# Hybrid attention and recurrence layer: output rows 8 to 11 taken into the fill, other buffers and queues for the end, first keys loaded earlier

## The chip, the cores and the metric

The kernel runs on one core of one Trainium2 chip. The metric is the device time of one execution in microseconds (us). The core has TensorE (PE), VectorE (DVE), ScalarE (ACT), GpSimd (POOL) and SyncE (SP), each with an instruction order that is fixed when the program is built. Before the change every DMA of the kernel is issued by SP, one after the other.

## What is computed

One layer of a decoder trunk over 2048 tokens of width 1024, in float32. Eight heads of differential attention and a gated linear recurrence (RG-LRU) run side by side; their outputs, 1024 wide each, go through one output projection.

```python
h = rmsnorm(x, pre_norm_g[l])
proj = jnp.einsum('bsd,de->bse', h, w_in[l])
q, k, v, g_attn, x_lru, g_lru = jnp.split(proj, SPLIT_POINTS, axis=-1)
...
    p = jax.nn.softmax(jnp.where(causal, s, -jnp.inf), axis=-1)
    w = p[:, :, 0] - lam * p[:, :, 1]
    outs.append(jnp.einsum('bhqk,bkhe->bqhe', w, v[:, :end].astype(jnp.float32)))
...
o = rmsnorm(o, subln_g[l]) * (1.0 - lam_init)
y_attn = o.reshape(B, S, ATTN_WIDTH).astype(x.dtype) * jax.nn.silu(g_attn)
xc = causal_depthwise_conv(x_lru, conv_w[l], conv_b[l])
hr = rg_lru(xc, w_r[l], b_r[l], w_i[l], b_i[l], lru_lambda[l])
y_lru = hr.astype(x.dtype) * jax.nn.silu(g_lru)
y = jnp.einsum('bse,ed->bsd', jnp.concatenate([y_attn, y_lru], axis=-1), w_out[l])
x = x + rmsnorm(y, post_norm_g[l])
```

## The kernel before

Every large product splits its float32 operands into a high and a low part and takes three matmuls of 128x512 (high by high, low by high, high by low). The work comes in stages, for the first half of the tokens (A) and the second (B): projections, the recurrence (`lru_run`, whose last piece is called as `end()`), and attention over four pairs of query rows (`range(0, 4)`, then `range(4, 8)`). Queries, keys, values, gates and the outputs `ya_s` (attention) and `yl_s` (recurrence) go through DRAM.

`attention` (L591) is a loop over slots. A slot belongs to a unit (head h, pair pr, tile t, component c), 128 of them in B, and twelve more slots follow the last unit. In a slot the code writes down, in this order: loads (keys L599, queries L615, values, gates), the exponentials of the unit (L679, ACT), then a mix of the next unit's score matmuls (L640) with their maxima (DVE), transposes of weights ("T", L711, whose low part `wl` is made by DVE), products with values ("V", L734) and **fill**, and at last the steps of the norm of a head and block j of 512 rows: `norm1` to `norm6`, "N1" to "N6" (L742 to L783). These steps are a square sum on PE (`pm`, L756), small operations on DVE (`f`), a trip through DRAM that spreads the result over the partitions (`r_s`, `rb`), a product on POOL (L779) and the store to `ya_s` (L782).

Fill is other PE work that comes from a generator, so many matmuls a slot: `FA` = 10 in A (projections of the second half), `FB` = 8.25 in B. B's fill is the output projection, `fill_out` (L1018), in 49 groups of 24 matmuls (L1045). A group (r, nh, i) multiplies the rows 128 i to 128 i + 127 of the recurrence's (r = 1) or attention's (r = 0) output by one half (nh = 0 left, nh = 1 right) of the columns of `w_out`. The order is (1,0), (1,1) for 16 rows each, then (0,0), (0,1) for the rows 0 to 7 that attention A has finished, then (0,1) of row 8. At the change from one set to the next, 8 pieces of weights are loaded (L947, two buffers) and split on POOL. All groups use one PSUM bank (`ps_f`). Partial sums go to DRAM (`part_s`) and come back (`part`, `yv`). When the right half of a row i below 8 is added (L1055), `finish` (L962) normalises the row of 1024 columns in the buffer `yv` (one buffer), adds x and stores it.

What is left stands in `p3`: the right halves of rows 9 to 15 and the left halves of rows 8 to 15 (`right` L1103, `left` L1110, matmuls L1095), with left weights that are loaded by SP into two buffers (L1120) and split between the right halves of rows 9, 10 and 11.

Memory pools lie on a left and a right side of SBUF; a tile in memory that another pool has given up waits for its last reader. A scheduler, which puts instructions mostly in the order in which the code gives them, fixes each engine's order, so a DMA can stand some rows away from its place in the code.

Of the kernel before, what the change touches and what calls it, by code (L numbers as in the profile page):

```python
# [8 lines left out]
F32 = mybir.dt.float32  # L9
# [34 lines left out]
def hymba_kernel(  # L44
# [342 lines left out]

    lightA = [light("k", 0), light("q", 0), light("g", 0)]
# [12 lines left out]
    with tc.tile_pool(name="ps_p", bufs=4, space=PSUM) as ps_p:  # L401
# [161 lines left out]
        with tc.tile_pool(name="lruA", bufs=2) as lp, tc.tile_pool(name="ps_g", bufs=1, space=PSUM) as ps_g:  # L563
# [3 lines left out]
            for job in jobs[5:]:  # L567
# [16 lines left out]
                pos += 2  # L584
            end()
    pA.close()

    def attention(prs, kv_p, e_p, a_p, ps_s, ps_w, ps_o, nsb, fill, per_slot, kbufs, vbufs, p1bufs):  # L591
        NS = len(prs)
        nmax = (prs[-1] + 1) * 256
        kst, vst, qst, gst, lch, wts = {}, {}, {}, {}, {}, {}

        def load_k(h, j):
            t = kv_p.tile([P, 2, CH], F32R, tag="ks", name="ks", bufs=kbufs)
            for e in range(2):
                nc.sync.dma_start(out=t[64 * e:64 * e + 64].bitcast(F32), in_=k_s[h][j][:, e])  # L599
            kst[h, j] = t  # L600

        def load_v(h, j):
            c0 = (h % 4) * P
            t = a_p.tile([P, 2, 4, P], F32R, tag="vs", name="vs", bufs=vbufs)
            nc.sync.dma_start(
                out=t.bitcast(F32).rearrange("p e t c -> p (e t) c"),
                in_=v_s[h // 4][j][:, :, :, c0:c0 + P].rearrange("p e t c -> p (e t) c"),
            )
            vst[h, j] = t[:, 0], t[:, 1]

        def load_q(h, pr):
            t0 = (pr % 2) * 256
            t = kv_p.tile([P, 2, 2, 256], F32R, tag="qs", name="qs", bufs=2)
            for r in range(2):
                nc.sync.dma_start(  # L615
                    out=t[64 * r:64 * r + 64].bitcast(F32), in_=q_s[h][pr // 2][:, :, :, t0:t0 + 256],
                )
            qst[h, pr] = t[:, 0], t[:, 1]

        def load_g(h, j):  # L620
            t = a_p.tile([P, CH], F32, tag="gt", name="gt", bufs=2)
            nc.sync.dma_start(out=t, in_=g_s[h][j])
            gst[h, j] = t


        def pieces(u):
            n = (2 * u[1] + u[2] + 1) * P
            return n, [(c0, min(n, c0 + SP)) for c0 in range(0, n, SP)]

        sc, negm, pex = {}, {}, {}  # L630

        def score_mm(u, pi):
            h, pr, t, c = u
            n, pcs = pieces(u)
            c0, c1 = pcs[pi]
            ps = ps_s.tile([P, SP], F32, tag="s", name="s")
            for b0 in range(c0, c1, CH):
                nk = max(256, min(CH, c1 - b0))
                for m, qq in enumerate(qst[h, pr]):
                    nc.tensor.matmul(  # L640
                        out=ps[:, b0 - c0:b0 - c0 + nk], lhsT=qq[:, c, t * P:(t + 1) * P],
                        rhs=kst[h, b0 // CH][:, c, 0:nk], start=(m == 0), stop=(m == 1),
                    )
            sc[u, pi] = ps

        def score_max(u, pi):
            n, pcs = pieces(u)
            c0, c1 = pcs[pi]
            if pi == 0:
                negm[u] = e_p.tile([P, 1], F32, tag="nm", name="nm", bufs=4)  # L650
            if pi == 0:
                sc[u, "mx"] = e_p.tile([P, 4], F32, tag="mx", name="mx", bufs=4)
            mx = sc[u, "mx"]
            s = sc[u, pi][:, 0:c1 - c0]
            if pi < len(pcs) - 1:
                nc.vector.tensor_reduce(out=mx[:, pi:pi + 1], in_=s, axis=AX.X, op=ALU.max)  # L656
                return

            nc.vector.tensor_tensor_reduce(
                out=s, in0=s, in1=mask16[:, CH - (c1 - c0):], scale=1.0, scalar=MASKED, op0=ALU.add, op1=ALU.max,  # L660
                accum_out=mx[:, pi:pi + 1],
            )
            nc.vector.tensor_reduce(out=negm[u], in_=mx[:, 0:pi + 1], axis=AX.X, op=ALU.max, negate=True)  # L663

        def score_exp(u):
            h, pr, t, c = u
            n, pcs = pieces(u)
            p = e_p.tile([P, nmax], F32, tag=f"p{c}", name=f"p{c}", bufs=(5, p1bufs)[c])
            pex[u] = p
            if (h, pr // 2) not in lch:  # L670
                lch[h, pr // 2] = e_p.tile([P, 4, 2], F32, tag="lch", name="lch", bufs=3)
            if c == 0 and len(pcs) > 1:
                sc[u[:3]] = e_p.tile([P, 2, 4], F32, tag="ls", name="ls", bufs=3)
            for pi, (c0, c1) in enumerate(pcs):
                if len(pcs) == 1:
                    acc = lch[h, pr // 2][:, (2 * pr + t) % 4, c:c + 1]
                else:
                    acc = sc[u[:3]][:, c, pi:pi + 1]
                nc.scalar.activation(  # L679
                    out=p[:, c0:c1], in_=sc.pop((u, pi))[:, 0:c1 - c0], func=AF.Exp, bias=negm[u], accum_out=acc,  # L680
                )

        def combine(h, pr, t):

            n, pcs = pieces((h, pr, t, 0))
            l2 = lch[h, pr // 2][:, (2 * pr + t) % 4, :]
            if len(pcs) > 1:
                nc.vector.tensor_reduce(
                    out=l2, in_=sc.pop((h, pr, t))[:, :, 0:len(pcs)], axis=AX.X, op=ALU.add,
                )  # L690
            rr = e_p.tile([P, 2], F32, tag="rr", name="rr", bufs=3)
            nc.vector.reciprocal(out=rr[:, 0:1], in_=l2[:, 1:2])
            nc.vector.scalar_tensor_tensor(
                out=rr[:, 1:2], in0=l2[:, 0:1], scalar=neglam, in1=rr[:, 0:1], op0=ALU.mult, op1=ALU.mult,
            )
            p0, p1 = pex.pop((h, pr, t, 0)), pex.pop((h, pr, t, 1))
            nc.vector.scalar_tensor_tensor(  # L697
                out=p0[:, 0:n], in0=p1[:, 0:n], scalar=rr[:, 1:2], in1=p0[:, 0:n], op0=ALU.mult, op1=ALU.add,
            )
            wts[h, pr, t] = p0  # L700


        tw, po = {}, {}

        def transpose_w(h, pr, b):
            pw = ps_w.tile([P, CH], F32, tag="pw", name="pw")
            cells = [(2 * b, 0), (2 * b, 1), (2 * b + 1, 0), (2 * b + 1, 1)]
            if b == pr:
                cells.pop(2)
            for i, (kb, t) in enumerate(cells):  # L710
                nc.tensor.transpose(pw[:, i * P:(i + 1) * P], wts[h, pr, t][:, kb * P:(kb + 1) * P], ident)  # L711
            n = len(cells) * P
            wh = a_p.tile([P, CH], F32R, tag="wh", name="wh", bufs=WB)
            wl = a_p.tile([P, CH], F32R, tag="wl", name="wl", bufs=WB)
            nc.scalar.activation(out=wh[:, 0:n], in_=pw[:, 0:n], func=AF.Copy)  # L715
            nc.vector.tensor_tensor(  # L716
                out=wl[:, 0:n], in0=pw[:, 0:n], in1=wh[:, 0:n].bitcast(F32), op=ALU.subtract,
            )
            tw[h, pr, b] = (wh, wl)

        def values(h, pr, b, e):
            j = pr // 2
            if pr % 2 == 0 and b == 0 and e == 0:
                po[h, j] = ps_o.tile([P, CH], F32, tag="o", name="o")
            wh, wl = tw[h, pr, b]
            o0 = (pr % 2) * 256
            kb = 2 * b + e
            vh, vl = vst[h, kb // 4]
            if b == pr and e == 1:
                w0, w1, oo = 256, 384, o0 + P  # L730
            else:
                w0, w1, oo = 256 * e, 256 * e + 256, o0
            for m, (a, w) in enumerate(((vh, wh), (vl, wh), (vh, wl))):
                nc.tensor.matmul(  # L734
                    out=po[h, j][:, oo:oo + w1 - w0], lhsT=a[:, kb % 4, :], rhs=w[:, w0:w1],
                    start=(kb == 0 and m == 0), stop=(kb == 2 * pr + 1 and m == 2),
                )


        nrm = {}  # L740

        def norm1(h, j):  # L742
# [49 lines left out]
        for p in range(H * NS):  # L792
# [16 lines left out]
            if p:  # L809
                later(s0 - 4, "Q", h, pr)  # L810
# [354 lines left out]
```

## Time and profile before

| | |
|---|---|
| median of 3 runs | 2257.87 us (2254.19 to 2262.12) |
| profiled execution, own time | 2261.0 us |
| its span in the profile | 2259.2 us |
| mean granted clock of PE | 0.983 |
| recurrence A, then attention A | from about 300 and 603 us |
| attention B: first score to last transpose of weights | 1379.3 to 2123.4 us |
| first matmul of `p3` (L1095) to the last | 2160.0 to 2250.5 us |

The page gives busy times by engine and the costliest groups of instructions. A row of the waits reads: engine, line, what it waited for, then the sum, the number and the longest of the waits in us. A row of the windows gives a stretch, its length and the busy time of each engine with its number of instructions. Matmuls overlap in the records: one of 128x512 shows about 390 ns, and the next starts 0.23 us after it.

### The profile page before, as it was taken

To read this page: it belongs to the slowest core of one execution; us is meant where nothing else is said; L and a number is where in the kernel's file an instruction comes from. 1 tells how busy PE (TensorE), PEld (TensorE's weight loads), DVE (VectorE), ACT (ScalarE), POOL (GpSimd) and SP (SyncE) were. 2 spreads that over 40 slices of the span, in tenths; PEclk is the share of its full clock that TensorE was granted. 3 is DMA by queue.
4 is the path that set the end of the run, shared out by engine and by line. 5 is a ranking of instruction groups with operands and counts; after the bars stand their busy time and mean duration, and the time that the engine had idled before them with its cause. 6 is when DMAs were issued, how large, how long until landed. Compare 5 with 4: busy or idle time off the path is not lost. (4 is left out here: it accounts for less than half of the span.)

```text
span 2259.2 us, 31702 instructions
## 1 busy us (share of the span) xinstructions
PE 2157.4 (95%) x11025; PEld 1792.9 (79%) x11025; DVE 1507.1 (67%) x3296; ACT 985.2 (44%) x2227; POOL 820.9 (36%) x773
## 2 busy tenths in 40 slices
PE   7999999999899999999999997999999998998888
PEld 7888888888678888888878775888788887887766
DVE  6531145546576767677347776888888887898775
ACT  4211134444454434444226565666556554555211
POOL 1223044434411111111366553223543235355542
PEclk9999999999999999999999998999999999999899
DMA  6554332332567665664552207456465455654473
GB/s 213 148 155 149 106 98 80 101 95 82 142 171 206 165 173 167 186 164 131 141 172 67 62 33 186 120 136 158 128 165 153 113 150 141 172 148 134 150 241 130
DMA packets 346497, 317.93 MB, mean 141 GB/s; under 512 B 20257, under 2 KB 278370, under 8 KB 346338
## 3 DMA queue, kind: packets, MB, share of 16 engines
q1 hardware_dynamic: 346338, 315.91, 50.0%
q8 instruction: 87, 1.43, 0.3%
q14 instruction: 72, 0.59, 0.1%
HBM read 221.41 MB, written 94.44 MB: 140 GB/s over the span
## 5 line engine op out<-in xcount | busy, mean ns | idle before, releaser
L227 PE MATMUL ps<-hh,whi 128*128 128x512 f32 (+1 forms) x1456 | 564.3, 388 | 0.0
L227 PE MATMUL ps<-hh,wlo 128*128 128x512 f32 (+1 forms) x1456 | 563.7, 387 | 0.0
L227 PE MATMUL ps<-hl,whi 128*128 128x512 f32 (+1 forms) x1456 | 562.5, 386 | 0.0
L679 ACT ACTIVATE p<-s,nm 128x512 f32<-128x512 f32 (+3 forms) x640 | 392.1, 623 | 342.1 <-DVE nm L663 295.4
L199 POOL TENSOR_TENSOR wlo<-wraw,whi 128x1024 fp32r<-128x1024 f32 x88 | 222.5, 2528 | 524.7 <-PE ps L227 187.6
L640 PE MATMUL s<-ks,qs 128*128 128x512 f32 (+2 forms) x1280 | 370.3, 387 | 29.8 <-DMA ks<-k_s 14.2
L656 DVE TENSOR_REDUCE mx<-s 128x1 f32<-128x512 f32 x384 | 258.6, 685 | 90.4 <-PE s L640 89.4
L227 PEld LDWEIGHTS ps<-hl,whi 128*128 128x128 f32 x1456 | 275.8, 189 | 51.6
L227 PEld LDWEIGHTS ps<-hh,wlo 128*128 128x128 f32 x1456 | 275.4, 189 | 51.2
L227 PEld LDWEIGHTS ps<-hh,whi 128*128 128x128 f32 x1456 | 276.0, 190 | 50.5
L640 PEld LDWEIGHTS s<-ks,qs 128*128 128x128 f32 x1280 | 213.0, 191 | 87.6 <-ACT p L679 44.2
L715 ACT ACTIVATE wh<-pw 128x512 fp32r<-128x512 f32 (+1 forms) x288 | 160.0, 577 | 164.1 <-PE pw L711 161.3
L70 POOL TENSOR_SCALAR yh<-yraw 128x256 fp32r<-128x256 f32 x196 | 95.0, 501 | 358.1 <-PE f L1045 357.8
L734 PE MATMUL o<-wh,vs 128*128 128x256 f32 (+1 forms) x1152 | 220.3, 283 | 0.6 <-ACT wh L715 0.6
L734 PEld LDWEIGHTS o<-wh,vs 128*128 128x128 f32 x1152 | 193.9, 192 | 18.5 <-ACT wh L715 2.6
L716 DVE TENSOR_TENSOR wl<-pw,wh 128x512 fp32r<-128x512 f32 (+1 forms) x288 | 185.9, 654 | 31.6 <-ACT wh L715 29.7
L697 DVE SCALAR_TENSOR_TENSOR p<-p,rr,p 128x128 f32<-128x128 f32 (+15 forms) x128 | 184.0, 1437 | 2.9
L711 PE MATMUL pw<-ident,p 128*128 128x128 f32 x1088 | 172.5, 275 | 8.5 <-DVE wl L716 6.3
L1045 PE MATMUL f<-woh,yh 128*128 128x512 f32 x392 | 161.7, 413 | 14.1 <-DVE yv L1055 7.6
L734 PE MATMUL o<-wl,vs 128*128 128x256 f32 x576 | 164.6, 286 | 5.5 <-DVE wl L716 5.0
L711 PEld LDWEIGHTS pw<-ident,p 128*128 128x128 f32 x1088 | 134.9, 141 | 42.2 <-issue 8.2
L1045 PE MATMUL f<-wol,yh 128*128 128x512 f32 x392 | 162.2, 414 | 0.0
(165 smaller groups left out, 3286.9 us busy)
## 6 DMA issues: line engine op xcount, KB each, us to landing
wraw<-in_w_in_dram SPq DMA_DIRECT2D x96, 512.0 KB, 4.7
qs<-q_s SPq DMA_DIRECT2D x128, 256.0 KB, 4.8
vs<-v_s SPq DMA_DIRECT2D x48, 512.0 KB, 5.1
ks<-k_s SPq DMA_DIRECT2D x96, 256.0 KB, 5.5
xt<-in_x_dram SPq DMA_DIRECT2D x32, 512.0 KB, 4.1
k_s<-hilo SPq DMA_DIRECT2D x64, 256.0 KB, 3.4
q_s<-hilo SPq DMA_DIRECT2D x64, 256.0 KB, 3.5
v_s<-hilo SPq DMA_DIRECT2D x32, 512.0 KB, 4.4
```

Of the source, the lines that this page charges most:

```text
L70: nc.gpsimd.tensor_scalar(out=hi, in0=src, scalar1=1.0, scalar2=1.0, op0=ALU.mult, op1=ALU.mult)
L199: nc.gpsimd.tensor_tensor(out=lo, in0=src, in1=hi.bitcast(F32), op=ALU.subtract)
L227: nc.tensor.matmul(out=ps[:, t0:t0 + n], lhsT=a[:, k, :], rhs=b[:, k, t0:t0 + n], start=(k == 0 and m == 0), stop=(k == KC - 1 and m == 2),)
L640: nc.tensor.matmul(out=ps[:, b0 - c0:b0 - c0 + nk], lhsT=qq[:, c, t * P:(t + 1) * P], rhs=kst[h, b0 // CH][:, c, 0:nk], start=(m == 0), st ...
L656: nc.vector.tensor_reduce(out=mx[:, pi:pi + 1], in_=s, axis=AX.X, op=ALU.max)
L679: nc.scalar.activation(out=p[:, c0:c1], in_=sc.pop((u, pi))[:, 0:c1 - c0], func=AF.Exp, bias=negm[u], accum_out=acc,)
L697: nc.vector.scalar_tensor_tensor(out=p0[:, 0:n], in0=p1[:, 0:n], scalar=rr[:, 1:2], in1=p0[:, 0:n], op0=ALU.mult, op1=ALU.add,)
L711: nc.tensor.transpose(pw[:, i * P:(i + 1) * P], wts[h, pr, t][:, kb * P:(kb + 1) * P], ident)
L715: nc.scalar.activation(out=wh[:, 0:n], in_=pw[:, 0:n], func=AF.Copy)
L716: nc.vector.tensor_tensor(out=wl[:, 0:n], in0=pw[:, 0:n], in1=wh[:, 0:n].bitcast(F32), op=ALU.subtract,)
L734: nc.tensor.matmul(out=po[h, j][:, oo:oo + w1 - w0], lhsT=a[:, kb % 4, :], rhs=w[:, w0:w1], start=(kb == 0 and m == 0), stop=(kb == 2 * pr ...
L1045: nc.tensor.matmul(out=ps, lhsT=a[:, k, :], rhs=b, start=(k == 0 and m == 0), stop=(k == 7 and m == 2),)
```

## The change

1. `attention` becomes a generator: it asks for the first keys and queries, yields, and then goes on as before. `attention_of` opens its pool and takes this first step; it is called ahead of the last `end()` of each recurrence. The pool of A's keys moves to the right side, where the projections' `pA` is closed earlier.
2. The fill of B is 9.4 a slot instead of 8.25, and ends with four groups (0,1,8) to (0,1,11), after row 7. Each waits, without holding up the slots, until the last head's "N6" of its block has been written down. They add the partial sum and store the right half back to `part_s`; the rows are finished in `p3`.
3. `yv` gets two buffers in a pool of its own.
4. In `p3` the left weights are loaded by ACT's DMA queue into eight buffers, the high part is made by ACT and the low part by DVE. The rights of rows 12 to 15 come first, then left 12, 8, 13, 9, 14, 10, 15, 11. The first half of `finish` moves from `right` to `left`. The pool lies on the right side; its split rows have five buffers instead of six.

```diff
+        for h, j in early:
+            load_k(h, j)
+        load_q(0, prs[0])
+        yield
+        e_p, a_p, ps_s, ps_w, ps_o, fill = pools
...
+                    elif r == "wait":
+                        nf = 0
...
+            gen = attention(range(4, 8), kv_p, pools, 4 * CH // SP, lambda s: 9.4 if s > 1 else 6, 6, 5, 1)
+        next(gen)
...
+            pA.close()
+            attA = attention_of("A")
             end()
-    pA.close()
...
         p1.close()
+        attB = attention_of("B")
         end()
...
-        groups = [(r, nh, i) for r, nh in wsets for i in range((8, 16)[r])] + [(0, 1, 8)]
+        v_p = pb.enter_context(tc.tile_pool(name="rowB", bufs=2, side="right"))
+        groups = [(r, nh, i) for r, nh in wsets for i in range((8, 16)[r])] + [(0, 1, i) for i in range(8, 12)]
...
+                if ysp is None:
+                    while (H - 1, i // 4) not in ya_done:
+                        yield "wait"
+                    ysp, parts = load_y(r, i)
...
-                if r == 0 and nh == 1:
+                if r == 0 and nh == 1 and i < 8:
                     nc.vector.tensor_tensor(out=yv[:, CH:], in0=ps, in1=part, op=ALU.add)
-                    ends[i] = finish(f_p, i, yv, 1, 1, nc.gpsimd if i < FE else nc.vector)
-                    if i < 8:
-                        ends.pop(i)()
+                    finish(f_p, i, yv, 1, 1, nc.gpsimd)()
...
+                        nc.sync.dma_start(
+                            out=part_s[1][i][:, CH:] if i >= 8 else part_s[0][i][:, 0:CH], in_=st,
+                        )
...
-        y_p = p3.enter_context(tc.tile_pool(name="y", bufs=2))
+        y_p = p3.enter_context(tc.tile_pool(name="y", bufs=2, side="right"))
...
+        def load_w0(k):
+            raw = y_p.tile([P, CH], F32, tag="woraw3", name="woraw3", bufs=8)
+            nc.scalar.dma_start(out=raw, in_=w_out2[k * P:(k + 1) * P, 0:CH])
+            return raw
+
+        def split_w0(k, raw):
...
+            nc.scalar.activation(out=hi, in_=raw, func=AF.Copy)
+            nc.vector.tensor_tensor(out=lo, in0=raw, in1=hi.bitcast(F32), op=ALU.subtract)
...
-        for i in range(9, 12):
...
-        for i in range(8, 16):
+        for i in range(12, 16):
...
             right(i)
...
+        for i in range(8, 12):
+            left(i + 4)
...
             left(i)
```

Three places show how the engines' orders move. The first is SP's order where attention A begins, before and after; `ks` and `qs` are the first keys and queries, `yl_s` the recurrence's stores, `vs` and `gt` values and gates, `hilo` stores of projected values:

```order
L343 DMA yl_s_201<-tg 128x512
L194 DMA wraw<-in_w_in_dram 128x8x128
L599 DMA ks<-k_s_0_92 64x1024 x2
L615 DMA qs<-q_s_0_60 64x4x256 x4
L599 DMA ks<-k_s_1_93 64x1024 x2
```

```order
L402 DMA ks<-k_s_0_92 64x1024 x2
L418 DMA qs<-q_s_0_60 64x4x256
L343 DMA yl_s_200<-tg 128x512
L418 DMA qs<-q_s_0_60 64x4x256 x3
L402 DMA ks<-k_s_1_93 64x1024
L343 DMA yl_s_201<-tg 128x512
```

The first keys stood behind the last store of the recurrence and stand ahead of its last two now.

The second is SP's order at the switch to the third set of output weights, (0,0), before and after. `woraw` are the weights, `yraw` rows of y, `part_s_15` the last partial sum of the set before; `k_s_0_116` to `k_s_2_118` are the keys of head 6, which u96 uses first:

```order
L947 DMA woraw<-in_w_out_dram 128x512
L955 DMA yraw<-ya_s_196 128x8x128
L947 DMA woraw<-in_w_out_dram 128x512 x6
L1066 DMA part_s_15_227<-fo 128x512
L947 DMA woraw<-in_w_out_dram 128x512
L955 DMA yraw<-ya_s_196 128x8x128
L599 DMA ks<-k_s_2_118 64x1024 x2
```

```order
L971 DMA woraw<-in_w_out_dram 128x512 x2
L585 DMA ya_s_198<-yt 128x512
L402 DMA ks<-k_s_0_116 64x1024
L971 DMA woraw<-in_w_out_dram 128x512 x2
L402 DMA ks<-k_s_0_116 64x1024
L402 DMA ks<-k_s_1_117 64x1024
L971 DMA woraw<-in_w_out_dram 128x512 x2
```

Before, the last keys of head 6 stood right behind the eight loads of weights; after, the loads stand between keys of the same head that are asked for earlier, and `k_s_2_118` comes 23 rows behind the last pair of loads.

The third is PE's order at the last `pm` of the kernel, the square sum of head 7 and block 3 (`norm2`), before and after. L1045 is fill (rows 6 to 8 behind `pm`), o (L734, after the change L537) products with values, ps_y (L1123 after the change) the matmuls of `p3`, the first of row 12:

```order
L734 MATMUL o<-wh,vs 128x128 x2
L734 MATMUL o<-wl,vs 128x128
L1045 MATMUL f<-woh_20086,yh 128x512
L1045 MATMUL f<-woh_20086,yl 128x512
L1045 MATMUL f<-wol_20087,yh 128x512
L756 MATMUL pm<-ones_235,sq 128x2 x4
L1045 MATMUL f<-woh_19911,yh 128x512
L1045 MATMUL f<-woh_19911,yl 128x512
```

```order
L537 MATMUL o<-wl,vs 128x128
L559 MATMUL pm<-ones_235,sq 128x2 x4
L1123 MATMUL ps_y<-woh_19202,yh_21597 128x512
L1123 MATMUL ps_y<-woh_19202,yl_21598 128x512
L1123 MATMUL ps_y<-wol_19203,yh_21597 128x512
```

Before, the fill of rows 6, 7 and 8 (72 matmuls) and then the rights of 9, 10 and 11 followed `pm`; after, the fill of rows 8 to 11 (96 matmuls) stands ahead of it, among the last products with values, and row 12 follows.

More of the change, by code (lines that the diff above doesn't have):

```diff
@@ L388, in hymba_kernel, with attention_of @@
+    def attention_of(half):
+        st = ExitStack()
+        kv_p = st.enter_context(tc.tile_pool(name="kv" + half, bufs=2, side="right"))
+        pools = []
+        if half == "A":
+            gen = attention(range(0, 4), kv_p, pools, NSA, lambda s: FA, 4, 4, 2)
+        else:
+            gen = attention(range(4, 8), kv_p, pools, 4 * CH // SP, lambda s: 9.4 if s > 1 else 6, 6, 5, 1)
+        next(gen)
+        return st, pools, gen
     lightA = [light("k", 0), light("q", 0), light("g", 0)]
@@ L898, in hymba_kernel @@
     with ExitStack() as pa:
-        kv_p = pa.enter_context(tc.tile_pool(name="kvA", bufs=2))
+        pkv, pools, run_attention = attA
+        pa.callback(pkv.close)
         e_p = pa.enter_context(tc.tile_pool(name="expA", bufs=2))
@@ L933, in fill_proj @@
                     yield "group"
-        attention(range(0, 4), kv_p, e_p, a_p, ps_s, ps_w, ps_o, NSA, fill_proj(), lambda s: FA, 4, 4, 2)
+        pools += [e_p, a_p, ps_s, ps_w, ps_o, fill_proj()]
+        for _ in run_attention:
+            pass
     pst.close()
@@ L1008, in hymba_kernel @@
     with ExitStack() as pb:
-        kvB_p = pb.enter_context(tc.tile_pool(name="kvB", bufs=2, side="right"))
+        pkv, pools, run_attention = attB
+        pb.callback(pkv.close)
         e_p = pb.enter_context(tc.tile_pool(name="expB", bufs=2, side="right"))
@@ L1023, in fill_out @@
             for g, (r, nh, i) in enumerate(groups):
+                if ysp is None:
+                    while (H - 1, i // 4) not in ya_done:
+                        yield "wait"
+                    ysp, parts = load_y(r, i)
+                    for p in parts:
+                        split(*p)
                 ps = ps_f.tile([P, CH], F32, tag="f", name="f")
@@ L1026, in fill_out @@
                 nxt = groups[g + 1] if g + 1 < len(groups) else None
-                if nxt:
+                ysp, parts = None, ()
+                if nxt and (nxt[0] or nxt[2] < 8 or (H - 1, nxt[2] // 4) in ya_done):
                     ysp, parts = load_y(*nxt[::2])
@@ L1030, in fill_out @@
                 c0 = nh * CH
-                if i >= 8 and r == 0:
-                    yv = f_p.tile([P, D], F32, tag="yv", name="yv", bufs=1)
-                    nc.sync.dma_start(out=yv, in_=part_s[1][i])
-                    part = yv[:, CH:]
-                    ys[i], yvs[i] = ysp, yv
-                elif r == 0:
-                    if nh:
-                        yv = f_p.tile([P, D], F32, tag="yv", name="yv", bufs=1)
+                if r == 0:
+                    if nh and i < 8:
+                        yv = v_p.tile([P, D], F32, tag="yv", name="yv")
                         nc.sync.dma_start(out=yv[:, 0:CH], in_=part_s[0][i][:, 0:CH])
@@ L1067, in fill_out @@
                 yield "group"
-        attention(
-            range(4, 8), kvB_p, e_p, a_p, ps_s, ps_w, ps_o, 4 * CH // SP, fill_out(),
-            lambda s: FB if s > 1 else 6, 6, 5, 1,
-        )
+        pools += [e_p, a_p, ps_s, ps_w, ps_o, fill_out()]
+        for _ in run_attention:
+            pass
     with ExitStack() as p3:
-        y_p = p3.enter_context(tc.tile_pool(name="y", bufs=2))
+        y_p = p3.enter_context(tc.tile_pool(name="y", bufs=2, side="right"))
         ps_y = p3.enter_context(tc.tile_pool(name="ps_y", bufs=6, space=PSUM))
@@ L1083, in load_ya @@
             nc.sync.dma_start(out=raw, in_=ya_s[i // 4][:, :, (i % 4) * P:(i % 4 + 1) * P])
-            yh = y_p.tile([P, 8, P], F32R, tag="yh3", name="yh3", bufs=6)
-            yl = y_p.tile([P, 8, P], F32R, tag="yl3", name="yl3", bufs=6)
+            yh = y_p.tile([P, 8, P], F32R, tag="yh3", name="yh3", bufs=5)
+            yl = y_p.tile([P, 8, P], F32R, tag="yl3", name="yl3", bufs=5)
             split3(yh, yl, raw, SY)
@@ L1101, in hymba_kernel, with begin, right @@
         w0 = []
-        def right(i):
+        def load_w0(k):
[3 more added lines that the diff above has]
+        def split_w0(k, raw):
+            hi = y_p.tile([P, CH], F32R, name=f"w3h{k}", bufs=1)
+            lo = y_p.tile([P, CH], F32R, name=f"w3l{k}", bufs=1)
+            nc.scalar.activation(out=hi, in_=raw, func=AF.Copy)
+            nc.vector.tensor_tensor(out=lo, in0=raw, in1=hi.bitcast(F32), op=ALU.subtract)
+            w0.append((hi, lo))
+        def begin(i):
             yvs[i] = y_p.tile([P, D], F32, tag="yv3", name="yv3", bufs=5)
             nc.sync.dma_start(out=yvs[i], in_=part_s[1][i])
+        def right(i):
             ps = out_mm(i, w1)
             nc.vector.tensor_tensor(out=yvs[i][:, CH:], in0=ps, in1=yvs[i][:, CH:], op=ALU.add)
-            ends[i] = finish(y_p, i, yvs[i], 2, 1 + (i == 15), nc.vector if FY else nc.gpsimd)
         def left(i):
+            ends[i] = finish(y_p, i, yvs[i], 2, 1 + (i == 11), nc.gpsimd)
             ps = out_mm(i, w0)
@@ L1113, in left @@
             ends.pop(i)()
-        load_ya(9)
-        load_ya(10)
-        for i in range(9, 12):
-            for k in ((0, 1, 2), (3, 4, 5), (6, 7))[i - 9]:
-                raw = y_p.tile([P, CH], F32, tag="woraw3", name="woraw3")
-                nc.sync.dma_start(out=raw, in_=w_out2[k * P:(k + 1) * P, 0:CH])
-                hi = y_p.tile([P, CH], F32R, name=f"w3h{k}", bufs=1)
-                lo = y_p.tile([P, CH], F32R, name=f"w3l{k}", bufs=1)
-                split3(hi, lo, raw, SW)
-                w0.append((hi, lo))
-            right(i)
-            load_ya(i + 2)
-        for i in range(8, 16):
+        raws = [load_w0(k) for k in range(8)]
+        for k, raw in enumerate(raws):
+            split_w0(k, raw)
+        load_ya(12)
+        load_ya(13)
+        begin(12)
+        begin(13)
+        for i in range(12, 16):
+            if i < 14:
+                load_ya(i + 2)
+                begin(i + 2)
+            elif i == 14:
+                load_ya(8)
+                begin(8)
+            right(i)
+        for i in range(8, 12):
+            left(i + 4)
+            if i < 11:
+                load_ya(i + 1)
+                begin(i + 1)
             left(i)
-            if i < 12:
-                right(i + 4)
-                if i + 6 < 16:
-                    load_ya(i + 6)
     pf.close()
```

532 lines of the change are left out of this document (265 added, 267 removed).

## Prediction

> **What bounds the kernel now.** Three views were read in this order: the page, the waits of TensorE (PE) stage by stage, and tables of windows. A "unit" below is one head, one pair of query rows, one tile and one component: attention B has 128 of them, numbered u0 to u127. The windows begin at the first score matmul of u64, u80 and so on.
>
> ```profile
> span 2259.2 us, 31702 instructions
> PE 2157.4 (95%) x11025; PEld 1792.9 (79%) x11025; DVE 1507.1 (67%) x3296; ACT 985.2 (44%) x2227; POOL 820.9 (36%) x773
> PE s L640 <- ACT p L679: 3.7, 10, 0.6
> PE s L640 <- DMA ks<-k_s: 3.5, 3, 1.6
> PE pw L711 <- DVE wl L716: 2.8, 2, 2.0
> ```
>
> PE is busy 95% of the span. The three rows of waits cover 1408.97 to 1900.5, the regular part of attention B: 10.0 us of waiting in 491.5. Both kernels have the same matmuls, so the change can win only what PE loses to waits and to the half clock, and it loses wherever it makes new ones. Here are the windows of attention B and the end (span, then PE, PEld, DVE, ACT, POOL, the granted clock, DMA):
>
> ```profile
> 1719.26:1761.23 41.97, 40.42 (x251) 34.90 (x250) 32.90 (x74) 24.56 (x67) 14.74 (x21) 1.00 0.73 184
> 1808.23:1852.31 44.08, 41.89 (x253) 36.20 (x254) 35.80 (x79) 25.44 (x70) 15.68 (x23) 1.00 0.71 177
> 1900.52:1950.91 50.39, 42.36 (x252) 36.68 (x250) 36.62 (x82) 23.48 (x66) 17.71 (x25) 0.90 0.71 187
> 1950.91:1998.45 47.54, 47.14 (x275) 39.40 (x274) 42.06 (x95) 28.10 (x79) 15.67 (x26) 1.00 0.47 127
> 1998.45:2041.00 42.55, 41.90 (x252) 35.55 (x251) 36.59 (x83) 22.95 (x64) 29.08 (x36) 1.00 0.58 172
> 2041.00:2123.40 82.40, 72.59 (x395) 60.71 (x395) 72.52 (x164) 40.06 (x111) 40.09 (x54) 0.92 0.42 130
> 2187.40:2250.50 63.10, 63.04 (x265) 50.81 (x265) 36.48 (x92) 7.96 (x22) 17.73 (x12) 0.97 0.41 143
> 2250.50:2259.20 8.70, 0.00 (x0) 0.00 (x0) 4.12 (x13) 0.72 (x2) 1.26 (x1) 0.61 0.30 121
> ```
>
> In the first two PE is full. The third holds one large stall. The sixth (u120 to the last transpose of weights) has PE and VectorE (DVE) waiting for each other. The seventh is 265 output matmuls on end: 63.10 / 265 = **0.238 us** is what a 128x512 matmul takes when PE is full.
>
> **The change part by part.** The sum is made against the profiled execution, whose own time is 2261.0, that is 3.1 above the median of 2257.87; the span ends 1.8 earlier.
>
> *First keys and queries asked for earlier.* Waits of PE where attention A and B begin:
>
> ```profile
> PE s L640 <- DMA ks<-k_s: 2.8, 1, 2.8
> PE s L640 <- issue: 1.2, 1, 1.2
> ```
>
> In A, the keys and half the queries now stand ahead of the recurrence's last two stores on SP's queue, and PE's first scores stand 68 matmuls earlier: the 2.8 go, I take **-2.7**. What comes late next is the stores, which only later rows read. Bounds: -4.5 (with the clock that sags behind a gap) to +2 (two stores held up behind loads that wait for a buffer). In B only half a set of queries moves ahead of one store, so I take the wait of 1.2 as gone: **-1.2**, bounds -3 and 0.
>
> *Denser fill, 8.25 to 9.4 a slot.* By the order of PE, u8 to u103 hold 889 fill matmuls instead of 768: +121. Their price is read from two windows of equal shape with 55 and 65 fills:
>
> ```profile
> 1719.26:1761.23 41.97, 16.33 (x55) 9.82 (x55) 1.00 0.73 184
> 1808.23:1852.31 44.08, 17.97 (x65) 11.62 (x65) 1.00 0.71 177
> PE s L640 <- DMA ks<-k_s: 0.9, 1, 0.9
> PE s L640 <- ACT p L679: 0.4, 1, 0.4
> PE pw L711 <- DVE wl L716: 2.0, 1, 2.0
> PE f L1045 <- ACT fo L1065: 0.2, 1, 0.2
> ```
>
> Ten more fills made 2.11 us, 0.21 each; without the waits (the first two rows are those of the first window, 1.3 us, the others those of the second, 2.2) it is 0.12. The other end is 0.238. I take the middle, 0.18: 121 x 0.18 = **+21.8**, bounds +14.5 and +28.8. It is work moved, not added: it comes back in the last two terms, as far as PE isn't waiting there.
>
> *The stall at 1902.* The wait of PE, and SP's queue around it:
>
> ```profile
> PE s L640 <- DMA ks<-k_s: 7.9, 1, 7.9
> 1880.43 16.62 SPq L947 DMA_DIRECT2D woraw<-in_w_out_dram  x6
> 1903.52 1.30 SPq L599 DMA_DIRECT2D ks<-k_s  x2
> ```
>
> Six weight loads, which wait for buffers, held SP's queue for 16.62 us, and the keys behind them, for u96, were asked for at 1903.52. After, the denser fill brings this switch of weights (behind 768 fills) to about u83; its loads stand in pairs with keys between that are needed only at u96, and the keys that stalled stand 23 rows behind the last pair. The window that begins at 1900.52 (55 fills as that at 1719.26) took 50.39 instead of 41.97: **-8.4**. Bounds: -11 (the clock was 0.90 in it, so the next one profits) and 0, if the next switch, now at u104, stalls in its place.
>
> *From u104 to the last transpose of weights (172.5 us before, the fourth to sixth window).* After, 58 and 48 fills stand in the last two groups of eight instead of 65 and 113, and the rest of the stretch has none: DVE becomes the bound. It was busy for 42.06 + 36.59 + 72.52 = 151.2. Eight row finishes fall into it instead of five; one is made of these (name, count, busy and mean, idle before):
>
> ```profile
> L1055 DVE TENSOR_TENSOR yv<-f,part 128x512 f32<-128x512 f32 x5 | 3.4, 686 | 0.5 <-PE f L1045 0.5
> L980 DVE SCALAR_TENSOR_TENSOR xt<-yv,ss,xt 128x1024 f32<-128x1024 f32 x4 | 5.1, 1281 | 0.1
> L97 DVE SCALAR_TENSOR_TENSOR ss<-ss 128x1 f32<-128x1 f32 x12 | 4.1, 344 | 0.0
> L96 DVE TENSOR_SCALAR ss<-ss 128x1 f32<-128x1 f32 x12 | 3.2, 267 | 0.1
> L976 DVE TENSOR_TENSOR ss<-ss 128x1 f32<-128x1 f32 x5 | 1.7, 335 | 2.9 <-ACT junk L969 2.9
> ```
>
> 0.69 + 1.28 + 3 x 0.34 + 3 x 0.27 + 0.34 = 4.1 each, three of them 12.4; two additions of left halves (0.68 each) have gone earlier, so DVE has about 162 us. At its highest share so far (42.06 of 47.54, 72.52 of 82.40: 0.88) the stretch would last 184, without any pause 162. I take the middle, 0.94: 172.3, **-0.2**, bounds -10.5 and +11.6. The row buffer doubled belongs here: the next row's load no longer waits for the row before; it goes with the stalls on `yv` below.
>
> *From there to the end (2123.4 to 2259.2, 135.8 us before).* Waits of PE in it:
>
> ```profile
> PE f L1045 <- DVE yv L1055: 5.9, 2, 3.4
> PE ps_y L1095 <- DVE w3h L202: 2.5, 1, 2.5
> PE ps_y L1095 <- DVE w3l L203: 1.5, 1, 1.5
> PE f L1045 <- DVE f L762: 1.5, 1, 1.5
> ```
>
> These 11.4 us go: rows 8 to 11 have no finish behind them, and the left weights are split on ScalarE and DVE while PE is idle anyway. What covered the last head's norm goes too. Its chain before:
>
> ```profile
> 2129.74 1.05 PE L756 MATMUL pm<-ones,sq 128*128 128x2 f32 x8
> 2137.92 0.17 DVE L82 SCALAR_TENSOR_TENSOR f<-f 128x4 f32<-128x4 f32 x1
> 2138.12 0.32 SPq L769 DMA_DIRECT2D r_s<-f  x1
> 2143.57 1.54 POOL L779 TENSOR_TENSOR yt<-yt,rb 128x512 f32<-128x512 f32 x1 [0.41 <-DMA rb<-r_s]
> 2145.14 0.32 SPq L782 DMA_DIRECT2D ya_s<-yt  x1
> 2153.51 2.37 POOL L203 TENSOR_TENSOR yl<-yraw,yh 128x1024 fp32r<-128x1024 f32 x1 [4.03 <-DVE yh L202]
> ```
>
> From `pm` to the first rows split took 2129.74 to 2155.88, 26.1 us, beside 72 fill matmuls (rows 6 to 8). After, rows 8 to 11 stand ahead of `pm`, and behind it only row 12, which needs this chain: PE has nothing. DVE's steps, 7 us there among finishes, should take some 3.7 less: **22.4 us idle**. So the end is: some 4 for row 8 (its own input comes through the norm before), rows 8 to 11 with 96 x 0.238 = 22.8 and 23 value matmuls of half the width 2.8, the chain 22.4, the clock behind it 2.1 (below), 288 x 0.238 = 68.5, and 8.7 for the last row: 131.3, or **-4.5**. Bounds: -11 (row 8 ready, chain 18) and +5 (chain 26, row additions as late as before). The loads of the left weights on ScalarE's queue lie in the idle 22 us and cost nothing; without that cover they would cost at most the 4.0 of the `w3` rows.
>
> Clock, two windows of it:
>
> ```profile
> 1904.26:1914.50 10.24, 4.31 (x17) 4.14 (x18) 1.81 (x7) 1.79 (x6) 0.00 (x0) 0.50 1.04 242
> 2132.95:2136.36 3.41, 3.41 (x10) 2.63 (x9) 3.24 (x6) 0.72 (x2) 3.41 (x6) 0.50 0.68 203
> ```
>
> After the 7.9 us of waiting, PE worked 4.31 us at half speed: 2.15 lost, which is the 2.1 above. The second window follows a wait of only 1.5 us (`f` L762). The Trainium skill ("TensorE: Matmul & The Clock Gate", "Part 1: The HAM clock gate") says that the clock falls to half after at least one idle window of about 3.4 us. By that rule the long chain would cost the same 2, and waits of 1 to 3 us would cost nothing beyond themselves; the second row speaks against it.
>
> **Sum:** -2.7 - 1.2 + 21.8 - 8.4 - 0.2 - 4.5 = +4.8, so 2265.8 against 2261.0, and 2262.7 on the basis of the median: **2263 us**, +0.2%. Some 0.3%, or 6.8 us, is what a measurement of this kernel tells from no change: 2251.1 and 2264.6 are the borders.
>
> **Rivals.**
> 1. *Faster: the fill is what kept PE and DVE waiting.* For it speaks that in 2041 to 2123 DVE idled 9.9 us while PE was in fills, and that the pair of windows gives 0.12 without waits. Then DVE runs its 162 through (-10.3 beside the forecast) and fills cost 0.12 (-7.3): 2245. Against it: transposes and values stay in one order on PE, and each waits for DVE.
> 2. *Slower: the half clock in the stretch without fill.* From about u120 PE waits for DVE at every transpose; where these waits reach the 1.5 us of the row above, PE answers at half speed and DVE idles for it. DVE's share then stays at 0.88 as in 2041 to 2123, whose clock was 0.92: 184 instead of 172.3, or 2274. It decides from that length of wait. By the skill's rule it would have no chance, since no such wait reaches 3.4 us.
> 3. *The stall is only moved:* half of u108's queries now stands behind six weight loads of the next switch. Then the -8.4 falls away: 2271. Against it: those loads come in two pairs and two single ones, and u108 is some 25 us off.
>
> **How the numbers follow.** Forecast 0.40 (2254 to 2272: of it 0.28 within 0.3%, 0.10 slower, 0.02 faster); rival 1 0.28, all faster; rival 2 0.22, all slower; rival 3 0.10 (0.07 slower, 0.03 within, as other terms may make good). Faster 0.30, same 0.31, slower 0.39. All lower bounds at once would give far less than 2245, but they exclude each other in part, since fill that costs little leaves little to win later; so the range goes some 5 us below rival 1 and 7 above rival 2: 2240 to 2281.
>
> **What would show it.** Right: the wait for keys of 2.8 us at A's start and that of 7.9 us are gone; windows of eight units of attention B are 1 to 3 us longer up to u103; then DVE above 0.9 and PE below 0.85; one wait of `ps_y` near 22 us behind `pm`, and no wait on `yv` or `w3`. Wrong: fills that lengthen no window, a new wait for keys near weight loads, or a granted clock near 0.9 over u112 to the last transpose. The step that I trust least is the price of the stretch that DVE bounds.

## The result and the profile after

The changed kernel takes 2270.85 us (median of 5 runs, 2266.17 to 2274.15), the kernel before 2257.87 (5 runs too); the ratio is 1.0055, 95% interval 1.0036 to 1.0073. It is slower, by some 13 us, inside the range of 2240 to 2281, but 8 us above the forecast of 2263 and beyond the 0.3% within which that lay. The profiled execution took 2269.13 us, its span is 2267.3. The two spans differ by 8.1 us only, since the profile of before lay 3.1 above its median and that of after lies 1.7 below its own.

The page of the changed kernel, busy times by engine:

```profile
span 2267.3 us, 31758 instructions
PE 2148.0 (95%) x11025; PEld 1787.5 (79%) x11025; DVE 1493.1 (66%) x3287; ACT 988.6 (44%) x2235; POOL 826.5 (36%) x800
```

By the two pages PE and DVE are busy for 9.4 and 14.0 us less than before, ACT and POOL for 3.4 and 5.6 more, with the same 11025 matmuls; what grew is PE's idle time, by 17.5 us. Windows of the two kernels with the same cuts place it: u8 to u103, u104 to the last transpose, from there to the first `ps_y` (the matmuls of `p3`), the `ps_y`, and the rest behind the last matmul (length; PE, PEld, DVE, ACT, POOL, clock, DMA). Before:

```profile
1409.00:1950.90 541.90, 521.95 (x3064) 441.44 (x3063) 450.13 (x1029) 322.75 (x872) 213.76 (x295) 0.99 0.55 145
1950.90:2123.70 172.80, 161.93 (x917) 135.97 (x917) 151.47 (x341) 91.42 (x252) 85.15 (x115) 0.96 0.48 139
2123.70:2160.00 36.30, 28.94 (x119) 23.02 (x118) 24.99 (x53) 5.59 (x15) 24.67 (x26) 0.86 0.69 220
2160.00:2250.40 90.40, 86.33 (x361) 68.52 (x359) 59.45 (x125) 10.86 (x30) 30.38 (x19) 0.96 0.53 177
2250.40:2259.20 8.80, 0.04 (x1) 0.00 (x0) 4.15 (x13) 0.72 (x2) 1.26 (x1) 0.61 0.30 119
```

After:

```profile
1396.50:1957.50 561.00, 547.86 (x3186) 465.42 (x3185) 454.05 (x1034) 323.46 (x875) 238.45 (x347) 1.00 0.56 149
1957.50:2130.00 172.50, 151.93 (x858) 124.77 (x857) 153.47 (x382) 94.72 (x261) 71.47 (x85) 0.96 0.48 143
2130.00:2178.20 48.20, 26.91 (x130) 22.08 (x129) 7.15 (x19) 1.32 (x3) 18.66 (x33) 0.84 0.38 115
2178.20:2248.60 70.40, 68.25 (x288) 54.90 (x288) 46.87 (x81) 12.63 (x33) 33.03 (x20) 0.96 0.61 204
2248.60:2267.30 18.70, 0.01 (x1) 0.00 (x0) 12.68 (x36) 2.57 (x8) 6.21 (x5) 0.59 0.42 154
```

The first stretch begins 12.5 us earlier and is 19.1 longer. The second has 59 fewer matmuls on PE and lasts as long as before. The third is 11.9 us longer. The last two lines show what the prediction had not seen: 72 matmuls fewer make `ps_y` 20 us shorter, but 10 of these us come back behind the last matmul. The waits of PE after, first where attention A begins, then from the last transpose to the end:

```profile
PE s L443 <- DMA qs<-q_s: 0.5, 1, 0.5
```

```profile
PE ps_y L1123 <- DVE yh L202: 18.3, 1, 18.3
PE ps_y L1123 <- POOL yl L203: 2.2, 2, 1.7
PE f L1074 <- POOL yl L71: 1.1, 2, 0.7
PE f L1074 <- POOL yh L70: 0.9, 1, 0.9
PE pm L559 <- ACT sq L549: 0.7, 1, 0.7
PE f L1074 <- DVE fo L1089: 0.2, 1, 0.2
```

The waits for the first keys (2.8 us) and for `yv` and `w3` (9.9 us) are gone, and one of 18.3 us for row 12 stands there. In the timeline after, the first and the last of the eight left halves of `p3` look like this on DVE, ACT and POOL:

```profile
2210.57 0.69 DVE L1154 TENSOR_TENSOR yv<-ps_y,yv 128x512 f32<-128x512 f32 x1 [4.78 <-PE ps_y L1123]
2212.00 2.40 POOL L203 TENSOR_TENSOR yl<-yraw,yh 128x1024 fp32r<-128x1024 f32 x1 [10.78 <-DVE yh L202]
2212.05 2.36 DVE L1000 TENSOR_TENSOR ss<-ss 128x1 f32<-128x1 f32 x1 [0.19 <-ACT junk L993]
2218.72 0.68 DVE L1154 TENSOR_TENSOR yv<-ps_y,yv 128x512 f32<-128x512 f32 x1
```

```profile
2252.88 0.68 DVE L1154 TENSOR_TENSOR yv<-ps_y,yv 128x512 f32<-128x512 f32 x1
2253.66 0.63 ACT L993 ACTIVATE junk<-yv 128x512 f32<-128x512 f32 x1 [4.55 <-DVE yv L1154]
2257.56 1.28 DVE L1004 SCALAR_TENSOR_TENSOR xt<-yv,ss,xt 128x1024 f32<-128x1024 f32 x1
2258.76 0.68 DVE L1154 TENSOR_TENSOR yv<-ps_y,yv 128x512 f32<-128x512 f32 x1
```

From its addition to that of the next, a row takes 8.15 us at first and 5.88 at the end: addition, square on ACT, the small steps of the root, the product, all in DVE's fixed order. A left half takes PE 5.44 us. The first left half is added as soon as PE has made it. The next three steps are 8.15, 8.25 and 8.14 us long and put DVE 8.3 us behind PE; the last four, of 5.9 each, add 1.9. In those three steps a later row is split as well, and one small step of DVE, which took 0.16 us at 2254.42, where POOL had no row to split, took 2.30 to 2.40 beside POOL's part of the split. PE ended at 2248.6, and the last addition began 10 us later.

### The profile page after: what moved, and what is told of

The parts are those of the page before. It is cut to its first block, busy times and chain, and to the rows that moved or that the text cites. A ratio compares the mean times of both kernels' runs of the same rounds, so it can differ in the third digit from the quotient of the medians.

```text
span 2267.3 us, 31758 instructions
## 1 busy us (share of the span) xinstructions
PE 2148.0 (95%) x11025; PEld 1787.5 (79%) x11025; DVE 1493.1 (66%) x3287; ACT 988.6 (44%) x2235; POOL 826.5 (36%) x800
## 5 line engine op out<-in xcount | busy, mean ns | idle before, releaser
L227 PEld LDWEIGHTS ps<-hh,whi 128*128 128x128 f32 x1456 | 275.3, 189 | 50.4
L537 PE MATMUL o<-wh,vs 128*128 128x256 f32 (+1 forms) x1152 | 219.2, 283 | 3.2 <-ACT wh L518 1.4
L537 PEld LDWEIGHTS o<-wh,vs 128*128 128x128 f32 x1152 | 192.8, 191 | 19.8 <-ACT wh L518 2.7
L1074 PE MATMUL f<-woh,yh 128*128 128x512 f32 x416 | 168.2, 404 | 7.9 <-ACT fo L1094 4.6
L1074 PE MATMUL f<-wol,yh 128*128 128x512 f32 x416 | 168.3, 405 | 2.5 <-POOL wol L71 2.0
L1074 PE MATMUL f<-woh,yl 128*128 128x512 f32 x416 | 168.2, 404 | 0.4 <-POOL yl L71 0.4
L537 PE MATMUL o<-wl,vs 128*128 128x256 f32 x576 | 163.4, 284 | 2.4 <-DVE wl L519 2.0
```

What stands on the lines that cost most here:

```text
L227: nc.tensor.matmul(out=ps[:, t0:t0 + n], lhsT=a[:, k, :], rhs=b[:, k, t0:t0 + n], start=(k == 0 and m == 0), stop=(k == KC - 1 and m == 2),)
L537: nc.tensor.matmul(out=po[h, j][:, oo:oo + w1 - w0], lhsT=a[:, kb % 4, :], rhs=w[:, w0:w1], start=(kb == 0 and m == 0), stop=(kb == 2 * pr ...
L1074: nc.tensor.matmul(out=ps, lhsT=a[:, k, :], rhs=b, start=(k == 0 and m == 0), stop=(k == 7 and m == 2),)
```

## The experiments

The leading theory was that three separate things cost the time: fill that was moved out of a stretch where it was free, the norm chain of the last head without cover, and finishes back to back on DVE. The rival to each is that the time would only turn up elsewhere. A ratio is to the kernel before, timed beside the run on the same chip (medians 2259.07, 2259.0 and 2256.45 in the three groups of runs). The changed kernel was timed once, beside 2257.87, so differences from it are good to a few us only.

**Fill at 8.25 again.**

```diff
-lambda s: 9.4 if s > 1 else 6
+lambda s: 8.25 if s > 1 else 6
```

> The changed kernel with the fill of attention B back at 8.25 a slot. Theory (each matmul of fill moved ahead of u104 costs its full 0.23 us there, and comes back only in part, because the stretch from u104 to the last transpose is set by DVE and lasts about 172 us with or without it): the windows from u8 to u103 together about 24 us shorter than in the changed kernel, u104 to the last transpose 170 to 178, the rest some 14 longer for the 62 matmuls then left: 2257 to 2264, some 6 to 14 below the changed kernel. Rival (the denser fill is repaid in full and the loss sits in the end alone): 2268 to 2274, no difference that can be told from the changed kernel.

Measured: 2265.91 us, ratio to the kernel before 1.0034 [1.0023, 1.0046]: some 5 below the changed kernel, between the two expectations. By its profile u8 to u103 took 546.5 us, not 24 but 14.5 less than after; the stall for the keys of u96 was back, with a wait of 7.7 us (u96 to u103 took 50.4 us, after 45.5). The stretch from u104 took 170.2 with 251 fills; after had 172.5 with 192. So fill was free there, as the theory has it. But now 144 fill matmuls were left behind `pm`, twice the 72 of the kernel before, and PE waited 6.8 us there for their additions (`fo`).

**Right and left of a row following each other.**

```diff
...
+        rows = [12, 13, 14, 15, 8, 9, 10, 11]
...
+            if i >= 12:
+                right(i)
+            left(i)
```

> The changed kernel with another order of p3: right and left of a row follow each other (12, 13, 14, 15), then left 8 to 11. Theory (in the changed kernel eight finishes follow each other at 5.9 us of DVE chain against 5.4 us of matmuls, so the last addition comes 10 us behind the last matmul): the time from the last matmul to the end falls from 18.7 to about 9 to 11 us, and the whole to 2261 to 2264. Rival (the tail follows from the half clock and from DMAs, or the wait for the left weights takes its place): the end stays within 3 us, 2268 to 2274.

Measured: 2264.21 us, 1.0021 [1.0007, 1.0034], 6.6 below the changed kernel. The windows of `ps_y` and of what follows it:

```profile
2181.60:2252.70 71.10, 69.28 (x288) 55.84 (x288) 55.47 (x100) 14.84 (x38) 39.31 (x23) 0.95 0.67 219
2252.70:2263.10 10.40, 0.00 (x0) 0.00 (x0) 6.01 (x17) 0.72 (x2) 1.48 (x2) 0.74 0.40 149
```

PE's 288 matmuls take about as long as in the changed kernel (71.1 and 70.4 us), and 10.4 us stand behind them instead of 18.7. The first four finishes, and the splits among them, now have a right half beside them; the chain of finishes on DVE was the cause. What the splits alone cost in it was read from the rows above, and no run took them away.

**Only the early keys, on the kernel before.** The edit is part 1 of the change, alone.

```diff
+            attA = attention_of("A")
             end()
...
+        attB = attention_of("B")
         end()
```

> The kernel before with nothing but the early keys and queries (generator, pool of A's keys on the other side, pA closed earlier). Theory (the first scores of A no longer wait for keys, and those of B for queries): attention A and B begin earlier by 5.5 and another 2 to 3 us, so 2249 to 2253, 6 to 9 below the kernel before. Rival (part of the 12 us by which B begins earlier in the changed kernel's profile is chance, and the terms are those of the prediction, 2.7 and 1.2): 2253 to 2256.

Measured: 2252.76 us, 0.9960 [0.9945, 0.9975], 6.3 below the median of before. That is more than the 3.9 of the prediction and at the small end of the 6 to 9 that the profile of after suggested.

**Rows 9, 10 and 11 behind the last `pm`.**

```diff
+            pm_done.add((h, j))
...
-                    while (H - 1, i // 4) not in ya_done:
+                    while (H - 1, i // 4) not in ya_done or (i >= 9 and (H - 1, 3) not in pm_done):
...
```

> The changed kernel with rows 9, 10 and 11 of the last fill held back until the last square sum pm has been written down, so that they cover its norm chain. Theory (PE idles 20 us there, and 72 matmuls are 16.7 us): the wait of ps_y falls from 18.3 to 2 to 5 us, the products with values lose some of their cover (2 to 4 us): 2256 to 2262. Rival (the DVE chain of the finishes sets the end whatever PE does, or the transposes' wl and wh take the place as a wait): a gain of under 5 us, 2266 to 2271.

Measured: 2255.46 us, 0.9980 [0.9969, 0.9991], 15.4 below the changed kernel. Its waits of PE from the last transpose on:

```profile
PE ps_y L1124 <- POOL yl L203: 3.9, 2, 2.0
PE ps_y L1124 <- issue: 1.7, 1, 1.7
PE f L1075 <- DVE fo L1090: 1.3, 1, 1.3
PE f L1075 <- POOL yh L70: 0.9, 1, 0.9
PE f L1075 <- POOL yl L71: 0.4, 1, 0.4
```

The 18.3 have gone. The products with values, which lost those rows as cover, cost nothing that can be seen: from the last transpose to `pm` it is 11.0 us instead of 29.8, with 68 fewer fill matmuls (16 us at 0.238).

**Both repairs.** The last two edits together.

> Rows 9 to 11 behind the last pm, and right and left of a row following each other: the two repairs together. Theory (the wait for the norm chain and the chain of finishes behind the last matmul are two separate losses): the gains of 15 and 6.6 add up, 2247 to 2251, with 9 to 11 us from the last matmul to the end. Rival (the finishes' chain on DVE bounds the end of the kernel from the first left on, so that either repair alone frees the same time): 2253 to 2257.

Measured: 2248.53 us, 0.9943 [0.9928, 0.9958]. The sum of the two gains would be 2248.9, and 10.5 us stand behind the last matmul: they are separate losses.

**Fill at 8.75.**

```diff
-lambda s: 9.4 if s > 1 else 6
+lambda s: 8.75 if s > 1 else 6
```

> The changed kernel with fill of 8.75 a slot. Theory (the stretch from u104 to the last transpose is bounded by DVE and lasts 170 to 173 us with 192 fills as with 251, so fill that stands there is free, while each ahead of u104 costs 0.12 to 0.2 us): some 66 fewer fills up to u104 make 8 to 13 us, nothing is given back behind: 2258 to 2263. Rival (8.25 gave 5 us only, and less fill before u104 is repaid behind): 2266 to 2271.

Measured: 2243.44 us, 0.9925 [0.9908, 0.9941]: 27 below the changed kernel, more than either theory gave. Windows of its fill alone (L1074): u8 to u103, to the last transpose, to `pm`, to the first `ps_y`; first after, then at 8.75:

```profile
1396.50:1957.50 561.00, 250.44 (x889) 157.91 (x889) 1.00 0.56 149
1957.50:2130.00 172.50, 55.15 (x192) 33.90 (x192) 0.96 0.48 143
2130.00:2159.80 29.80, 23.15 (x96) 17.71 (x96) 1.00 0.34 105
2159.80:2178.20 18.40, 0.00 (x0) 0.00 (x0) 0.59 0.45 131
```

```profile
1401.90:1943.70 541.80, 235.47 (x817) 145.10 (x817) 1.00 0.55 148
1943.70:2118.00 174.30, 75.90 (x264) 46.48 (x264) 0.99 0.53 153
2118.00:2129.80 11.80, 6.50 (x24) 4.26 (x24) 1.00 0.44 145
2129.80:2153.20 23.40, 19.12 (x73) 14.43 (x73) 0.93 0.59 180
```

72 matmuls fewer made the first stretch 19.2 us shorter, 0.27 each: PE was busy for 530.9 us in it instead of 547.9, which is 0.24 each, and the other 2.2 us are waits. 72 more made the second 1.8 longer, and as the generator was then not yet empty, its last three rows fell behind `pm` by themselves: 18.0 us less ahead of it, 5.0 more behind. Both steps of the theory's mechanism held; its size, 8 to 13 us, failed because a fill cost more than its 0.12 to 0.2 and because it took the order behind the last transpose to stay.

**The two repairs and 8.75.**

> The two repairs and fill of 8.75 a slot. Theory: the gains of all three add up, 2270.9 - 15 - 6.6 - 8 to 13: 2236 to 2242, below both kernels. Rival (once rows 9 to 11 cover the chain, PE is the bound to the end and less fill before u104 comes back there): 2246 to 2251, as with the repairs alone.

Measured: 2236.02 us, 0.9887 [0.9869, 0.9906], below both kernels and called the best version from here on: 23.0 us under the 2259.0 of before on the same chip. Beside fill of 8.75 alone it is 7.4 better, about what the pairs gave by themselves. The cover that the rows give was already there. The first two windows of its profile, all engines:

```profile
1398.00:1940.20 542.20, 531.46 (x3114) 451.23 (x3113) 446.61 (x1030) 320.94 (x870) 222.46 (x323) 1.00 0.55 148
1940.20:2117.10 176.90, 162.55 (x932) 135.60 (x932) 157.45 (x377) 94.85 (x261) 85.46 (x107) 0.98 0.52 151
```

The second is 5.6 us longer than with both repairs and 9.4 a slot (171.3), where the pair without the repairs differs by 1.8; so the 72 fills there are cheap (0.03 to 0.08 us each) rather than free.

**A second row buffer, on the kernel with early keys alone.**

```diff
+        v_p = pb.enter_context(tc.tile_pool(name="rowB", bufs=1, side="right"))
...
-                        yv = f_p.tile([P, D], F32, tag="yv", name="yv", bufs=1)
+                        yv = (f_p, v_p)[i % 2].tile([P, D], F32, tag="yv", name="yv", bufs=1)
```

> The kernel before with early keys and queries (2252.8) and, in addition, a second row buffer: rows of even and odd number have one each. Theory (the second buffer lets the next row's left half be loaded ahead, so the waits of the fill for yv, 1.7 and 5.9 us, go): 2244 to 2249. Rival (the fill waits for the addition on DVE, which stands behind the finish of the row before, not for the buffer): 2251 to 2254, no change.

Measured: 2256.71 us, 0.9987 [0.9974, 1.0000], no gain over 2252.76. Among the waits of PE from 2030 us on, first without and then with the buffer:

```profile
PE f L1071 <- DVE yv L1081: 7.7, 4, 3.1
```

```profile
PE ps_y L1121 <- DMA yraw<-ya_s: 12.6, 1, 12.6
PE f L1072 <- DVE yv L1082: 2.6, 2, 1.8
```

The waits for `yv` did fall, from 7.7 to 2.6, so the theory was right about them; but in SP's new order the row that `p3` begins with is asked for at 2149.62, behind the store of a finished row, instead of 2137.59, and PE waits for it. Neither theory had that.

**Left weights on SP's queue, in the best version.**

```diff
-            nc.scalar.dma_start(out=raw, in_=w_out2[k * P:(k + 1) * P, 0:CH])
+            nc.sync.dma_start(out=raw, in_=w_out2[k * P:(k + 1) * P, 0:CH])
```

> The version with the two repairs and fill of 8.75 (2236.0), its left weights loaded by SP's queue instead of ScalarE's. Theory (the loads lie under the last rows of the fill and only have to be issued, so the queue is worth what SP loses in issuing eight loads ahead of the rows that row 12 needs, some 3 us): 2236 to 2241. Rival (the loads wait on SP for memory that attention gives up and hold the rows of row 12 behind them): 2243 to 2250.

Measured: 2241.13 us, 0.9928 [0.9911, 0.9945], 5.1 above the best version, at the upper end of the theory. The two were timed on different chips; by their ratios they are 0.41% or some 9 us apart. The first wait of `ps_y` is 6.1 us in its profile and 1.3 in that of the best version. ScalarE's queue is worth 5 to 9 us there. Whether it pays in the changed kernel itself, where row 12 is waited for 18.3 us anyway, was not run.

**8.25 up to u103, 10.4 from there, in the best version.**

```diff
-lambda s: 8.75 if s > 1 else 6
+lambda s: 6 if s < 2 else 8.25 if s < 104 else 10.4
```

> The two repairs with fill of 8.25 a slot up to u103 and 10.4 from there. Theory (fill ahead of u104 costs 0.2 to 0.27 us each, behind it nothing up to some 264): 48 fewer ahead make 10 to 13 us, but the keys of u96 stand behind the loads of the weights again as in the kernel before, 5 to 8 us: 2230 to 2235. Rival (0.12 us each, and at 264 fills the stretch from u104 is already full, so more of it lengthens it): 2238 to 2246.

Measured: 2245.39 us, 0.9956 [0.9941, 0.9971]: the time that the rival gave. Its first window, its fill in the first two, and the wait at u96:

```profile
1397.80:1945.40 547.60, 524.42 (x3066) 442.56 (x3064) 451.22 (x1029) 323.35 (x873) 221.05 (x303) 0.99 0.53 142
1397.80:1945.40 547.60, 223.00 (x769) 135.52 (x769) 0.99 0.53 142
1945.40:2131.20 185.80, 88.75 (x310) 55.81 (x311) 0.97 0.54 155
PE s L443 <- DMA ks<-k_s: 7.7, 1, 7.7
```

The stall for keys is back: PE waits 12.8 us for keys in the first window, against 4.5 in the best version, and then works some 5 us at half clock. PE is busy for 7.0 us less, and the window is still 5.4 longer. So 48 fewer fills gain nothing, but not because a fill costs only 0.12, as the rival had it: without the half of those 5 us, PE's busy time would differ by some 9.6, or 0.20 a fill. The rival's other half held: against the best version, 46 more than 264 fills behind u104 lengthen that stretch by 8.9 us, or 0.19 each (11.5 and 0.25 against 8.75 without the repairs). It is full at about 264.

## Why the prediction came out as it did

The kernel was called unchanged within 0.3%, with slower as the single most likely side (0.39), and is 0.55% slower. That the time lies in the range is in part luck: terms that were too small on both sides cancel, and 2270.85 lies nearest to the times of rivals 2 and 3 (2274 and 2271), whose mechanisms did not come. The parts, by the two profiles:

| part | predicted, us | measured, us |
|---|---|---|
| first keys of A | -2.7 | -5.5 |
| first keys of B | -1.2 | -3.6 |
| denser fill and the stall at 1902 | +13.4 | +19.1 |
| u104 to the last transpose | -0.2 | -0.3 |
| from there to the end | -4.5 | +1.7 |

The rest of the 8.1 is 2.4 us that the changed profile gained in the first 85 us, where nothing was changed, and 1.0 in attention A and the recurrence. Both are taken for chance. The 2.4 are missing in two later profiles whose code there is the same (fill at 8.75, and rows 9 to 11 behind `pm`), which bears this out for them.

*First keys.* Too small, and beyond the bound of -4.5 for A and of -3 for B in this one profile. The wait for the keys went, and with it, by the waits of PE, some of the wait of `pv` (2.2 to 1.4 us): scores that come earlier fill it. In the other profiles with early keys A gains some 3 to 6 us, counted from 85 us on, so the 5.5 are near the upper end. The measured worth of both is 6.3 by medians, against 3.9.

*Denser fill.* The price of 0.18 was too low: between 8.75 and 9.4 a fill took 0.24 us of PE's busy time, the upper end that the prediction named, and 0.27 with the waits. The pair of windows that gave 0.12 was not of equal shape: by its rows the second has ten fills more but only two matmuls more in all (251 and 253). Four products with values and up to four transposes, of about 0.1 us each (eight of the products in a row took 0.95), fall outside it, and with these put back, PE's 40.42 and 41.89 us give an estimate of 0.19 to 0.24 a fill. The 0.238 itself is a little high, since its window of 265 matmuls had a clock of 0.97; a left half of 24 took 5.44 us in the changed kernel, 0.227 each. The 17 extra fills at u96 came with a window 4.9 shorter, so the stall did go (-8.4 predicted), as the version with 8.25 and that with 8.25 and 10.4 confirm by bringing it back. The +19.1 is the dearest reading: the four other profiles with 769 fills took 545.0 to 548.1 us, against 541.9 before, and by them it is +12.9 to +16.0, with the predicted +13.4 inside. There the dearer fill is paid for by more waits for keys that went (11.5 us before and 2.2 after in u8 to u103) than the one stall of the prediction.

*The stretch that DVE bounds.* Right to 0.1 us, but by two errors that cancel: DVE had 153.5 us to do, not 162, and reached a share of 0.89, not 0.94. All five additions of left halves had gone from it, not two, and the small steps on `f` were shorter (10.1 us instead of 13.0). It takes 172.5 us with 192 fills, 170.2 with 251 and 174.3 or 176.9 with 264; that PE does not set it there was the core of the mechanism, and also why moving fill out of it loses. That DVE sets it rests on its share; no run changed DVE's work there by itself.

*The end.* This is the step that failed: "8.7 for the last row" was taken over from before. It became 18.7, +10.0. The prediction had counted 288 matmuls and the idle PE, and not that eight finishes in a row make a chain on DVE that is longer than the left halves of 5.44 us beside it: 8.1 to 8.3 us a row for the first three steps, with a row's split and POOL beside them, and 5.9 for the others. With right halves between the finishes 10.4 us remained. The chain behind `pm` was predicted as 22.4 us idle and measured as 18.3 and two waits for `yl`, 2.2 together. Rows 8 to 11 with the wait ahead of them were predicted as 29.6 and measured as 29.8. The clock behind it was half for 5.3 us, in which PE was busy for 3.55 us; half of that, 1.8, was lost, where 2.1 had been said.

*The rivals.* Rival 1 (fill in PE's waits at 0.12) is refuted by the 0.24 to 0.27. Rival 2 asked for a clock near 0.9 and a stretch of 184 us from u104; it was 0.96 and 172.5. Rival 3 (queries of u108 behind weight loads) did not show in the changed kernel: PE has no wait for `qs` from u104 on. The rule of the Trainium skill that a full idle window of about 3.4 us halves the clock ("TensorE: Matmul & The Clock Gate", "Part 1: The HAM clock gate") again does not agree with this case: after a wait of PE of 1.53 us (2120.16 to 2121.69) the clock was half from 2122.09 on for 3.41 us, though PE had been busy for 1.63 of the 3.41 us ahead of that.

What stays open: why the first stretch differs by up to 6 us between profiles with the same 768 or 769 fills (541.9 to 548.1), and with it how much of the +19.1 is the change.

## What to carry to other kernels

In this kernel fill had its full price where PE was the bound and almost none where PE was not: count what each stretch can take at little cost, keep that much for it, and let a last piece stand behind the final dependent chain. When matmuls are taken out of a tail, look at the chain of small operations for each row of output; as soon as it is longer than the matmuls beside it, it sets the end, and pairing rows with other work hides it. Time a step at each place in the row's timeline, since the same small step can be much longer beside another engine's work. A change that takes away a wait in a queue of DMAs also reorders that queue, so the next thing behind it has to be looked up.

## What the runs showed of the hardware

The eleven small operations on `f` of one norm took 2.0 us in the changed kernel, 0.16 each, with POOL idle (2159.85 to 2161.98), and 6.1 us before (2132.03 to 2138.09, with steps of a finish between them), where single ones took up to 1.21 while POOL split and multiplied rows beside them. Likewise the step of `ss` on 128x1 took 0.16 us at 2254.42, where POOL had no row to split, and 2.36 at 2212.05 beside POOL's `yl`. No run here took POOL's work away, so that POOL is the cause is read from the traces alone. Changing the rate of fill by 7%, from 9.4 to 8.75, moved the whole kernel by 27 us, more than any other single edit did.
